# All up units of the feed-forward layers but each layer's first as seven block products

## The chip, the cores and the metric

The kernel runs on one NeuronCore of a Trainium2 chip. The metric is the time of one launch on the device in microseconds: the median of several runs, the profiled execution aside.

## The reference

A trunk of two encoder layers on 512 tokens of width 1024, all in float32. The token mixers (a gated linear recurrence with latent attention in the first layer, differential attention in the second) are not touched here. Each layer ends with a gated feed-forward part of 2816 hidden features:

```python
def swiglu(h, w_gate, w_up, w_down):
    return (jax.nn.silu(h @ w_gate) * (h @ w_up)) @ w_down

for layer in range(DEPTH):                      # DEPTH = 2
    ...
    x = x + mix
    x = x + swiglu(rmsnorm(x, norm_ffn[layer]), ffn_w_gate[layer], ffn_w_up[layer], ffn_w_down[layer])
return rmsnorm(x, final_norm)
```

## The kernel before

**Numbers.** Every float32 operand of a big product is held as two parts, hi and lo, and a product is three matmuls (`mm3`, L335 to L337): hi by hi, the weight's hi by the activation's lo, the weight's lo by the activation's hi. Features lie on partitions and tokens run along a row, so an activation tile is 128 features by 512 tokens.

**Weights.** `weight_plan` is a list of entries in the order of use; an entry is up to 512 rows by 256 columns of a weight matrix, loaded into a tile `raw` (two buffers) by SyncE's DMA queue and split by `_split` (L292 on ScalarE, L293 on VectorE) into `whi` and `wlo` (four buffers each). Asking for entry i with `weight` first writes the splits up to entry i + 2, and each split writes the load of the next free entry behind it. A buffer is written again only when those who read its last content are done: raw is free when both halves of the split have read it, whi and wlo when TensorE has.

**The feed-forward part.** `ffn_hidden` goes over the 22 hidden blocks of 128 features in groups of 8, 8 and 6 (GROUPS). In a group it takes pairs of blocks b, b + 1: first a unit for gate (256 columns), then one for up. Behind each group `projection` multiplies the group's hidden features by their rows of the down weights and adds to the residual (L667). There are two forms of a unit:

- An ordinary unit (`features`) has two PSUM banks. Per entry (two in a unit) it takes two column blocks by four row blocks by three matmuls of 512 tokens: 48 matmuls. Evacuation of up: L1044 (by the norm), L1045 (by the silu of gate), then oph (L343 on ScalarE) and opl (L344 on VectorE), per block of 512.
- A seven-product unit (`seven`) sees weights and activations as two by two blocks and takes seven block products instead of eight (PRODUCTS), each of 128 by 128 by 256 tokens. Per entry that is 7 products by 2 pairs of row blocks by 3 matmuls of 256 tokens, 84 matmuls in a unit. Its weights are split by `_split7`: sums of weight blocks on VectorE (`wsum`, L306 to L308), then hi on ScalarE and lo on VectorE (L314, L315) of both the plain blocks (`whi`, `wlo`, 128x768) and the sums (`shi`, `slo`, 128x1024). The first three products of an entry use the plain blocks, the other four the sums. The products land in four of the eight PSUM banks; the evacuation puts them together (L403 on ScalarE into `tu`, L404 to L408 on VectorE into a tile `cz`), multiplies by the norm (L1034) and, for up, by the silu of gate (L1050), and makes hi and lo of the two blocks (L343 and L346 on ScalarE, L344 and L347 on VectorE). For gate, ScalarE's L1039 is the silu.

Which form a unit takes is decided by `seven(w, b)`:

```python
def seven(w, b):

    return b > 0 if w == "gate" else b % 4 == 2
```

so gate has seven products everywhere but at b = 0, and up at b = 2, 6, 10, 14 and 18. For b = 0 both are ordinary, because the norm is not there yet.

**Order.** TensorE's instructions stand in the order in which the code writes them. Those of the other engines are put in order by the scheduler of the language, from its own idea of when each can run; each engine then works through its list in that order.

Of the kernel before, what the change touches and what calls it, by code (L numbers as in the profile page):

```python
# [49 lines left out]
def weight_plan():  # L50
    plan = []
    for p in range(2):
        for base in (512, 1024, 0, 2048, 1536):
            plan += [("ab_in", k, 4, base + 256 * p, 256) for k in (0, 4)]
    for c in (2560, 2816, 3072):
        plan += [("ab_in", k, 4, c, 256) for k in (0, 4)]
    plan += [("uq", k, 1, 0, 768) for k in range(3)]
    plan += [("ukv", k, 1, 0, 1024) for k in range(2)]
    for k in (0, 4):
        plan += [("ab_out", k, 4, 256 * j, 256) for j in range(4)]  # L60
    plan += ffn_plan(0)
    for hp in range(4):
        for base in (0, 1024, 2048):
            plan += [("c_in", k, 4, base + 256 * hp, 256) for k in (0, 4)]
    for k in (0, 4):
        plan += [("c_out", k, 4, 256 * j, 256) for j in range(4)]
    plan += ffn_plan(1)
    return plan


def seven(w, b):

    return b > 0 if w == "gate" else b % 4 == 2


def ffn_plan(l):
    plan = []
    for g0, gn in GROUPS:
        for b in range(g0, g0 + gn, 2):
            for w in ("gate", "up"):  # L80
                plan += [("seven" * seven(w, b) + w + str(l), k, 4, 128 * b, 256) for k in (0, 4)]
        if l == 0 or g0 + gn < FFN // 128:
            for j in range(4):
                plan += [(f"down{l}", g0 + k, min(4, gn - k), 256 * j, 256) for k in range(0, gn, 4)]
        else:
            for ch in range(2):
                plan += [("down1", g0 + k, 2, 512 * ch, 512) for k in range(0, gn, 2)]
    return plan
# [56 lines left out]
class Kernel:  # L145
# [871 lines left out]
    def ffn_hidden(self, l, g0, gn, xg, stats, sums):  # L1017


        nc = self.nc  # L1020
        hop = self.operand("f", (0, 1))
        parts, make = sums
        for b in range(0, gn, 2):
            zs = []

            def gate(i, ps):
                if not zs:
                    zs.append(self.s4("cz"))
                z = zs[0][:, 1 - i, :]
                nc.vector.tensor_mul(z, ps[:], self.R[:])  # L1030
                nc.scalar.activation(z, z, AF.Silu)

            def by_norm(c):
                nc.vector.tensor_mul(c[:], c[:], self.R[:].unsqueeze(1).broadcast_to([128, 2, 512]))  # L1034

            def gate7(c):
                by_norm(c)
                for i in range(2):
                    nc.scalar.activation(c[:, i, :], c[:, i, :], AF.Silu, scale=2.0 * i - 1.0)  # L1039
                zs.append(c)  # L1040

            def up(i, ps):
                u = self.s2("u")
                nc.vector.tensor_mul(u[:], ps[:], self.R[:])  # L1044
                nc.vector.tensor_mul(u[:], u[:], zs[0][:, 1 - i, :])  # L1045
                self.hi_lo(u[:], *hop(b + i))

            def up7(c):
                by_norm(c)
                nc.vector.tensor_mul(c[:], c[:], zs[0][:])  # L1050
                self.hi_lo(c[:, 1, :], *hop(b))
                self.hi_lo(c[:, 0, :], *hop(b + 1), scale=-1.0)

            if self.R is None:

                held = []

                def norm():
                    self.r = self.rms(stats[0], D)

                def release():
                    self.R = self.spread(self.r)
                    for h in held:
                        gate(*h)

                for m in range(2):
                    make(m)
                yield from self.features(f"gate{l}", 128 * (g0 + b), FULL, xg, lambda *h: held.append(h))
                for m in range(2, 4):
                    make(m)  # L1070
                yield from self.later(self.later(self.features(f"up{l}", 128 * (g0 + b), FULL, xg, up),
                                                 norm, steps=1), release, steps=4)
                continue
            for w, evac, evac7 in (("gate", gate, gate7), ("up", up, up7)):
                if seven(w, g0 + b):
                    yield from self.seven(f"seven{w}{l}", 128 * (g0 + b), parts, evac7)
                else:
                    yield from self.features(f"{w}{l}", 128 * (g0 + b), FULL, xg, evac)
        return hop
# [319 lines left out]
```

## Time and profile before

| | us |
|---|---|
| median of 3 runs | 1308.56 (1308.08 to 1309.05) |
| the profiled execution | 1309.75 |
| its span on the core | 1308.0 |
| TensorE busy | 1285.5 (98%) |
| VectorE busy | 967.9 (74%) |
| ScalarE busy | 612.2 (47%) |
| GpSimd busy | 164.8 (13%) |
| granted clock of TensorE, mean | 0.996 of full |

PE is TensorE's matmuls, PEld its weight loads, DVE VectorE, ACT ScalarE, POOL GpSimd, SP SyncE. The duration of a matmul in a timeline is longer than its distance from the next, since matmuls overlap in the array; VectorE's rows overlap a little too. How long a run of them takes is read from start to start, or from a stretch divided by its instructions.

### The profile page before, as it was taken

How to read it: one execution, taken by the hardware profiler on the slowest of the kernel's cores; microseconds unless marked ns; L12 is line 12 of the kernel's file. 1: busy time of each engine (PE TensorE's matmuls, PEld its weight loads, DVE VectorE, ACT ScalarE, POOL GpSimd, SP SyncE). 2: the span in 40 equal slices, each digit the busy share in tenths (PEclk: the TensorE clock that was granted, in tenths of full speed). 3: DMA queues.
4: the chain of work that ended last, by engine and by line, in shares of the span. 5: the costliest groups of instructions: out<-in, count | busy, mean ns of one | idle time of the engine just before them, and what ended most of it. 6: DMA issues, size and time to landing. Idle time of an engine off the chain costs nothing.

```text
span 1308.0 us, 19724 instructions
## 1 busy us (share of the span) xinstructions
PE 1285.5 (98%) x7746; PEld 1146.3 (88%) x7746; DVE 967.9 (74%) x1575; ACT 612.2 (47%) x1060; POOL 164.8 (13%) x147
## 2 busy tenths in 40 slices
PE   7999999999999999999999999999989999999997
PEld 7898988888799899989988889888879989998996
DVE  4678498646998479748767888887789748865964
ACT  6554464744644234324354566665654323432442
POOL 0222232001200000000035223130310000000002
PEclk9999999999999999999999999999989999999999
DMA  6422123212233333332332221221123333333331
GB/s 197 129 66 65 51 68 107 72 33 56 74 113 114 97 97 98 113 97 83 104 105 81 81 65 49 65 65 50 49 86 108 113 97 97 97 114 97 101 110 65
DMA packets 111745, 115.34 MB, mean 88 GB/s; under 512 B 7786, under 2 KB 107812, under 8 KB 111652
## 3 DMA queue, kind: packets, MB, share of 16 engines
q1 hardware_dynamic: 110324, 112.11, 28.1%
q10 hardware_dynamic: 1328, 1.97, 0.5%
q8 instruction: 61, 1.00, 0.3%
q14 instruction: 32, 0.26, 0.1%
HBM read 111.97 MB, written 2.10 MB: 87 GB/s over the span
## 4 chain that ended last, share of the span: by engine, by line
PE 90%; DVE 3%; issue 3%; ACT 2%; POOL 1%; DMA 0%; POOLq 0%; ACTq 0%
PE mm L335 26%; PE mm L336 26%; PE mm L337 26%; PE o L869 3%; PE lv L734 2%; PE pt L859 1%; PE o L777 1%; PE sc L1205 1%; PE sc L1206 1%; DVE opl L347 1%; DVE wlo L293 1%; PE lv L768 1%; PE bc L469 1%; PE ot L509 0%; DVE xT L667 0%
## 5 line engine op out<-in xcount | busy, mean ns | idle before, releaser
L335 PE MATMUL mm<-oph,whi 128*128 128x512 f32 (+1 forms) x1208 | 452.8, 375 | 1.1 <-ACT whi L292 1.1
L336 PE MATMUL mm<-opl,whi 128*128 128x512 f32 (+1 forms) x1208 | 445.0, 368 | 0.9 <-DVE opl L347 0.9
L337 PE MATMUL mm<-oph,wlo 128*128 128x512 f32 (+1 forms) x1208 | 445.0, 368 | 0.0
L337 PEld LDWEIGHTS mm<-oph,wlo 128*128 128x128 f32 x1208 | 228.9, 189 | 38.4 <-DVE wlo L293 0.2
L336 PEld LDWEIGHTS mm<-opl,whi 128*128 128x128 f32 x1208 | 229.5, 190 | 36.3 <-DVE opl L347 1.3
L335 PEld LDWEIGHTS mm<-oph,whi 128*128 128x128 f32 x1208 | 229.5, 190 | 36.3 <-ACT whi L292 1.5
L292 ACT CAST whi<-raw 128x1024 fp32r<-128x1024 f32 (+1 forms) x130 | 131.2, 1012 | 197.5 <-PE mm L336 130.6
L293 DVE TENSOR_TENSOR wlo<-raw,whi 128x1024 fp32r<-128x1024 f32 (+1 forms) x130 | 155.0, 1195 | 83.5 <-ACT whi L292 83.1
L337 PE MATMUL mm<-th,slo 128*128 128x256 f32 x360 | 101.9, 283 | 0.0
L335 PE MATMUL mm<-th,shi 128*128 128x256 f32 x360 | 101.9, 283 | 0.0
L336 PE MATMUL mm<-tl,shi 128*128 128x256 f32 x360 | 101.9, 283 | 0.0
L314 ACT CAST shi<-wsum 128x1024 fp32r<-128x1024 f32 x60 | 62.4, 1049 | 70.5 <-DVE wsum L308 64.3
L488 POOL TENSOR_TENSOR sq<-sq,sq 128x512 f32<-128x512 f32 x24 | 37.1, 1546 | 441.8 <-ACT sq L494 440.5
L315 DVE TENSOR_TENSOR slo<-wsum,shi 128x1024 fp32r<-128x1024 f32 x60 | 73.3, 1224 | 15.2 <-ACT shi L314 15.1
L667 DVE TENSOR_TENSOR xT<-xT,mm 128x512 f32<-128x512 f32 x72 | 49.1, 684 | 37.6 <-PE mm L337 37.5
L851 ACT ACTIVATE p<-sc,mx 128x512 f32<-128x512 f32 x80 | 55.0, 691 | 45.6 <-DVE mx L849 41.0
L335 PE MATMUL mm<-whi,oph 128*128 128x256 f32 (+1 forms) x246 | 75.4, 306 | 0.0
L337 PE MATMUL mm<-whi,opl 128*128 128x256 f32 (+1 forms) x246 | 74.1, 301 | 0.0
L336 PE MATMUL mm<-wlo,oph 128*128 128x256 f32 (+1 forms) x246 | 74.0, 301 | 0.0
L314 ACT CAST whi<-raw 128x768 fp32r<-128x768 f32 x60 | 50.0, 834 | 41.6 <-PE mm L336 25.2
L335 PEld LDWEIGHTS mm<-th,shi 128*128 128x128 f32 x360 | 69.1, 192 | 0.0
L336 PEld LDWEIGHTS mm<-tl,shi 128*128 128x128 f32 x360 | 69.1, 192 | 0.0
(241 smaller groups left out, 2329.6 us busy)
## 6 DMA issues: line engine op xcount, KB each, us to landing
raw<-in_ffn_w_down_dram SPq DMA_DIRECT2D x42, 512.0 KB, 3.4
raw<-in_ffn_w_gate_dram SPq DMA_DIRECT2D x80, 256.0 KB, 3.0
raw<-in_ab_w_in_dram SPq DMA_DIRECT2D x24, 512.0 KB, 3.8
raw<-in_ffn_w_up_dram SPq DMA_DIRECT2D x24, 512.0 KB, 3.7
raw<-in_c_w_in_dram SPq DMA_DIRECT2D x24, 512.0 KB, 3.6
raw<-in_ffn_w_up_dram SPq DMA_DIRECT2D x40, 256.0 KB, 2.9
xs<-in_x_dram SPq DMA_DIRECT2D x8, 512.0 KB, 5.1
raw<-in_ab_w_out_dram SPq DMA_DIRECT2D x8, 512.0 KB, 3.4
```

Of the source, the lines that this page charges most:

```text
L292: self.nc.scalar.copy(h, r)
L293: self.nc.vector.tensor_sub(l, r, h.bitcast(F32))
L314: nc.scalar.copy(hi, src)
L315: nc.vector.tensor_sub(lo, src, hi.bitcast(F32))
L335: mm(ps, lhsT=lhs[0], rhs=rhs[0], start=first, stop=False)
L336: mm(ps, lhsT=lhs[0], rhs=rhs[1], start=False, stop=False)
L337: mm(ps, lhsT=lhs[1], rhs=rhs[0], start=False, stop=last)
L488: self.nc.gpsimd.tensor_add(acc[0][:], acc[0][:], s[:])
L667: nc.vector.tensor_add(self.x(j), self.x(j), ps)
L734: nc.tensor.matmul(ps[:, sl], lhsT=kc[:, sl], rhs=qc[:, sl], start=True, stop=True)
L851: nc.scalar.activation(p[:], ps, AF.Exp, bias=m[:], scale=scale, accum_out=l)
L869: self.nc.tensor.matmul(po[:, tb * 128:(tb + 1) * 128], lhsT=pt[:, s * 128:(s + 1) * 128], rhs=V[:, s // 2, c:c + 128], start=s == 0, stop ...
```

## The change

`seven` takes only b, and is true for b > 0, for up as for gate: in each layer the up units at b = 4, 8, 12, 16 and 20 become seven-product units as well. Their weight entries are loaded as two transfers of 256 KB in place of one of 512 KB and split by `_split7`.

```diff
-def seven(w, b):
-
-    return b > 0 if w == "gate" else b % 4 == 2
+def seven(b):
+
+    return b > 0
...
-                plan += [("seven" * seven(w, b) + w + str(l), k, 4, 128 * b, 256) for k in (0, 4)]
+                plan += [("seven" * seven(b) + w + str(l), k, 4, 128 * b, 256) for k in (0, 4)]
...
-                if seven(w, g0 + b):
+                if seven(g0 + b):
                     yield from self.seven(f"seven{w}{l}", 128 * (g0 + b), parts, evac7)
```

TensorE has ten times 84 matmuls in place of ten times 48. With more seven-product units the scheduler also orders VectorE's and ScalarE's lists otherwise around those that were there. In the rows that follow, an instruction is named by its line, its operation, the tile it writes and those it reads, with the numbers of the buffers.

First place: VectorE in the second group of the first layer, around the start of the evacuation of the last gate unit (b = 14). slo885 and slo891 are the sums' lo parts for the two entries of the up unit behind it. Before:

```order
L307 TENSOR_TENSOR wsum881_4940<-wsum881_4940,raw866_4858 128x2x128
L1045 TENSOR_TENSOR u876_4931<-u876_4931,cz856_4832 128x512
L308 TENSOR_TENSOR wsum881_4940<-wsum881_4940,raw866_4858 128x2x128
L306 TENSOR_TENSOR wsum887_4996<-raw872_4897 128x2x256
L344 TENSOR_TENSOR opl875_4916<-u876_4931,oph874_4915 128x512
L307 TENSOR_TENSOR wsum887_4996<-wsum887_4996,raw872_4897 128x2x128
L315 TENSOR_TENSOR slo885_4947<-wsum881_4940,shi884_4946 128x1024
L308 TENSOR_TENSOR wsum887_4996<-wsum887_4996,raw872_4897 128x2x128
L315 TENSOR_TENSOR wlo889_5001<-raw872_4897,whi888_5000 128x768
L315 TENSOR_TENSOR slo891_5003<-wsum887_4996,shi890_5002 128x1024
L404 TENSOR_TENSOR cz893_5052<-tu894_5053,mm877_4936 128x256
```

After, the same tiles are slo912 and slo918:

```order
L347 SCALAR_TENSOR_TENSOR opl903_5114<-cz899_5102,oph902_5113 128x512
L306 TENSOR_TENSOR wsum908_5123<-raw892_5000 128x2x256
L306 TENSOR_TENSOR wsum914_5179<-raw898_5057 128x2x256
L307 TENSOR_TENSOR wsum908_5123<-wsum908_5123,raw892_5000 128x2x128
L307 TENSOR_TENSOR wsum914_5179<-wsum914_5179,raw898_5057 128x2x128
L308 TENSOR_TENSOR wsum908_5123<-wsum908_5123,raw892_5000 128x2x128
L308 TENSOR_TENSOR wsum914_5179<-wsum914_5179,raw898_5057 128x2x128
L404 TENSOR_TENSOR cz920_5235<-tu921_5236,mm904_5119 128x256
L405 TENSOR_TENSOR tu921_5236<-tu921_5236,mm906_5121 128x256
L315 TENSOR_TENSOR slo912_5130<-wsum908_5123,shi911_5129 128x1024
L315 TENSOR_TENSOR slo918_5186<-wsum914_5179,shi917_5185 128x1024
```

Both slo stood ahead of the gate unit's evacuation and stand now behind its L404 and L405, which read the banks of that gate unit.

Second place: ScalarE at the end of that group, where the last up unit (b = 14) is evacuated and the down projection begins. oph909 (after: oph936) is the hi part of that unit's hidden blocks. Before:

```order
L403 COPY tu907_5165<-mm896_5064 128x256
L292 CAST whi916_5213<-raw905_5120 128x1024
L343 CAST oph909_5175<-cz906_5164 128x512
L346 ACTIVATE oph909_5175<-cz906_5164 128x512
L292 CAST whi921_5247<-raw915_5187 128x1024
L292 CAST whi924_5277<-raw918_5217 128x1024
```

After:

```order
L403 COPY tu934_5348<-mm923_5247 128x256
L1039 ACTIVATE cz920_5235<-cz920_5235 128x512 x2
L292 CAST whi940_5366<-raw929_5255 128x1024
L292 CAST whi943_5396<-raw932_5303 128x1024
L292 CAST whi948_5430<-raw942_5370 128x1024
L343 CAST oph936_5358<-cz933_5347 128x512
L346 ACTIVATE oph936_5358<-cz933_5347 128x512
```

The fifth split of the down projection (whi921, now whi948) stood behind the two halves of oph and stands now ahead of them.

Third place: VectorE at the same point. Before:

```order
L405 TENSOR_TENSOR tu907_5165<-tu907_5165,mm898_5066 128x256
L406 TENSOR_TENSOR uu908_5166<-tu907_5165,mm897_5065 128x512
L407 TENSOR_TENSOR cz906_5164<-uu908_5166,mm897_5065 128x256
L408 TENSOR_TENSOR cz906_5164<-uu908_5166,mm899_5067 128x2x256
L1034 TENSOR_TENSOR cz906_5164<-cz906_5164,R620_3215 128x1024
L1050 TENSOR_TENSOR cz906_5164<-cz906_5164,cz893_5052 128x1024
L344 TENSOR_TENSOR opl910_5176<-cz906_5164,oph909_5175 128x512
L347 SCALAR_TENSOR_TENSOR opl910_5176<-cz906_5164,oph909_5175 128x512
L293 TENSOR_TENSOR wlo922_5248<-raw915_5187,whi921_5247 128x1024
```

After:

```order
L405 TENSOR_TENSOR tu934_5348<-tu934_5348,mm925_5249 128x256
L406 TENSOR_TENSOR uu935_5349<-tu934_5348,mm924_5248 128x512
L407 TENSOR_TENSOR cz933_5347<-uu935_5349,mm924_5248 128x256
L408 TENSOR_TENSOR cz933_5347<-uu935_5349,mm926_5250 128x2x256
L293 TENSOR_TENSOR wlo941_5367<-raw929_5255,whi940_5366 128x1024
L1034 TENSOR_TENSOR cz933_5347<-cz933_5347,R620_3215 128x1024
L293 TENSOR_TENSOR wlo944_5397<-raw932_5303,whi943_5396 128x1024
L1050 TENSOR_TENSOR cz933_5347<-cz933_5347,cz920_5235 128x1024
L293 TENSOR_TENSOR wlo949_5431<-raw942_5370,whi948_5430 128x1024
L344 TENSOR_TENSOR opl937_5359<-cz933_5347,oph936_5358 128x512
L347 SCALAR_TENSOR_TENSOR opl937_5359<-cz933_5347,oph936_5358 128x512
```

The chain from the banks to opl ran without a break and holds now three splits of down weights. The first group of the first layer, and the first two of the second, stand in the same way at all three places; the third group has no split of down weights between its last L405 and its last opl.

## Rows read from the trace of the kernel before

**Rows 1.** The page, part 1 (busy time by engine) and part 4 (chain).

```profile
PE 1285.5 (98%) x7746; PEld 1146.3 (88%) x7746; DVE 967.9 (74%) x1575; ACT 612.2 (47%) x1060; POOL 164.8 (13%) x147
...
PE 90%; DVE 3%; issue 3%; ACT 2%; POOL 1%; DMA 0%; POOLq 0%; ACTq 0%
```

**Rows 2.** Busy times by stretch, first layer's feed-forward part; its first row names the columns.

```profile
core 0: us, PE busy (x) PEld busy (x) DVE busy (x) ACT busy (x) POOL busy (x), PEclk, DMA share, GB/s
357.23:387.47 30.24, 30.24 (x254) 30.23 (x253) 29.21 (x46) 14.59 (x21) 0.00 (x0) 1.00 0.41 122
462.07:472.15 10.08, 10.08 (x86) 10.07 (x85) 5.87 (x11) 3.43 (x5) 0.00 (x0) 1.00 0.17 54
472.15:483.05 10.90, 10.90 (x50) 9.01 (x49) 10.85 (x16) 5.20 (x7) 0.00 (x0) 1.00 0.42 128
...
534.27:544.35 10.08, 10.08 (x87) 10.08 (x86) 7.21 (x10) 4.58 (x6) 0.00 (x0) 1.00 0.49 158
544.35:587.89 43.54, 43.54 (x194) 36.04 (x193) 23.06 (x29) 10.19 (x11) 0.00 (x0) 1.00 0.33 97
```

**Rows 3.** Timeline of DVE, second group: start, duration, instruction, idle before and its end.

```profile
485.95 0.95 DVE L315 TENSOR_TENSOR wlo<-raw,whi 128x768 fp32r<-128x768 f32 x1
486.82 0.69 DVE L344 TENSOR_TENSOR opl<-u,oph 128x512 fp32r<-128x512 f32 x1
...
494.24 0.42 DVE L407 TENSOR_TENSOR cz<-uu,mm 128x256 f32<-128x256 f32 x1
494.57 0.69 DVE L408 TENSOR_TENSOR cz<-uu,mm 128x512 f32<-128x512 f32 x1
495.17 1.22 DVE L315 TENSOR_TENSOR slo<-wsum,shi 128x1024 fp32r<-128x1024 f32 x1
496.30 1.23 DVE L1034 TENSOR_TENSOR cz<-cz,R 128x1024 f32<-128x1024 f32 x1
```

**Rows 4.** Timeline of DVE around the end of the second group, at 544.35.

```profile
528.40 1.23 DVE L315 TENSOR_TENSOR slo<-wsum,shi 128x1024 fp32r<-128x1024 f32 x1
...
543.83 0.42 DVE L405 TENSOR_TENSOR tu<-tu,mm 128x256 f32<-128x256 f32 x1
544.28 0.69 DVE L406 TENSOR_TENSOR uu<-tu,mm 128x512 f32<-128x512 f32 x1
545.00 0.42 DVE L407 TENSOR_TENSOR cz<-uu,mm 128x256 f32<-128x256 f32 x1
545.34 0.68 DVE L408 TENSOR_TENSOR cz<-uu,mm 128x512 f32<-128x512 f32 x1
...
549.22 0.69 DVE L344 TENSOR_TENSOR opl<-cz,oph 128x512 fp32r<-128x512 f32 x1 [0.69 <-ACT oph L343]
```

**Rows 5.** Timeline of ACT at the same place.

```profile
549.83 1.05 ACT L292 CAST whi<-raw 128x1024 fp32r<-128x1024 f32 x1
```

**Rows 6.** The page: costliest groups (part 5) and DMA issues (part 6).

```profile
L314 ACT CAST shi<-wsum 128x1024 fp32r<-128x1024 f32 x60 | 62.4, 1049 | 70.5 <-DVE wsum L308 64.3
...
L314 ACT CAST whi<-raw 128x768 fp32r<-128x768 f32 x60 | 50.0, 834 | 41.6 <-PE mm L336 25.2
...
raw<-in_ffn_w_down_dram SPq DMA_DIRECT2D x42, 512.0 KB, 3.4
...
raw<-in_ffn_w_up_dram SPq DMA_DIRECT2D x40, 256.0 KB, 2.9
```

**Rows 7.** Timeline of PE at two of its waits, one in each layer.

```profile
340.33 0.50 PE L336 MATMUL mm<-opl,whi 128*128 128x512 f32 x1 [0.90 <-DVE opl L347]
...
962.68 0.80 PE L469 MATMUL bc<-cst,rt 128*128 128x128 f32 x2 [4.67 <-POOL rt L461]
```

**Rows 8.** Busy times by stretch at these two waits; columns as in rows 2.

```profile
338.00:342.00 4.00, 3.10 (x14) 2.24 (x13) 4.00 (x5) 2.52 (x4) 1.73 (x1) 1.00 0.43 131
...
963.00:965.00 2.00, 2.00 (x10) 1.90 (x10) 0.00 (x0) 0.15 (x1) 0.00 (x0) 0.50 0.00 0
...
967.00:969.00 2.00, 2.00 (x9) 1.54 (x9) 1.31 (x4) 1.62 (x3) 0.00 (x0) 0.86 0.00 0
```

## The prediction

> **What bounds the kernel now.** I read part 1 and the chain of the page first [rows 1]: TensorE is busy 98% of a span of 1308.0 us, 90% of the chain that ended last is PE, VectorE (DVE) is busy 74%, ScalarE (ACT) 47%. Then the feed-forward part unit by unit in the busy times by stretch [rows 2]. A unit there is 256 hidden columns of gate or of up. An ordinary unit is 48 matmuls of 512 columns in 10.90 us, 0.227 us each; a seven-product unit is 84 of 256 columns in 10.08 us, 0.120 us each (the view's own counts are one or two higher, since it counts those that reach over an edge). In both PE is busy for the whole stretch: it waits for nobody. But DVE is busy 29.21 of 30.24 us where three seven-product units stand in a row (gate, up, gate at 357), 10.85 of 10.90 in the unit at 472, and only 7.21 of 10.08 and 23.06 of 43.54 in the last unit of a group and in the down projection behind it. So PE is the bound, and in the middle of a group DVE is nearly one too.
>
> **What the change takes off PE.** Five up units in each layer (b = 4, 8, 12, 16, 20) turn from ordinary into seven-product units: ten times 10.90 - 10.08 = 0.82 us, **-8.2 us**, if PE goes on waiting for nobody. The first units of the layers stay ordinary, and no DMA is added in bytes (two transfers of 256 KB for one of 512 KB).
>
> **What it puts on DVE.** I price DVE's instructions by the distance from one start to the next where they stand close [rows 3]: 0.60 us for 128x512 (L306, L406, L408, L344, L347), 0.34 for 128x256 (L307, L308, L404, L405, L407), 0.87 for the 128x768 wlo, 1.13 for 128x1024 (slo, L293, L1034, L1050). Splitting one weight entry then costs 0.60 + 2 x 0.34 + 0.87 + 1.13 = 3.28 us in place of 1.13, and a unit has two entries. Evacuating an up unit costs 3 x 0.34 + 2 x 0.60 + 2 x 1.13 + 2 x 0.60 = 5.7 in place of 6 x 0.60 = 3.6; a gate unit 3.4. A pair of two seven-product units therefore asks 4 x 3.28 + 5.7 + 3.4 = 22.2 us of DVE in 2 x 10.08 = 20.16 us of PE. Before, every other pair had an ordinary up unit, 2 x 3.28 + 2 x 1.13 + 3.6 + 3.4 = 15.8 us in 20.98, and DVE caught up there. That breathing space is gone, up to the last unit of a group, whose DVE work is cheap since the next splits are those of down weights.
>
> ACT gets 0.83 + 1.05 us per entry [rows 6] for 1.05, at 47% busy: nothing by itself. Its place in the queue matters, below.
>
> **Where PE then waits.** The queues are in order, so I walked the changed order at the two places where the rows moved.
>
> First place: the last gate unit of groups 1 and 2 (b = 6 and 14). Before, slo of the following up unit's first entry was written ahead of that gate unit's evacuation; it ended at 529.6 [rows 4], and PE needs it 18 + 2 matmuls of 0.120 us into the up unit that begins at 534.27, at 536.7: 7 us to spare. Now slo912 stands behind L404 and L405 of the gate unit's evacuation, which wait for the gate unit's own end. Counted from L405 of the up unit before (released 0.52 us before that unit's end, as 543.83 against 544.35 [rows 2, 4]) to the end of slo912, DVE has L405, L406, wlo, slo, L407, L408, wlo, L1034, L1050, L344, L347, twice L306, L307 and L308, L404, L405 and slo912: 0.34 + 0.60 + 0.87 + 1.13 + 0.34 + 0.60 + 0.87 + 1.13 + 1.13 + 0.60 + 0.60 + 1.20 + 0.68 + 0.68 + 0.34 + 0.34 + 1.13 = 12.6 us, so it ends 12.1 us after that unit's end. PE needs it at 10.08 + 2.40 = 12.5. Without any idle it is met by 0.4. But in this stretch DVE waits 0.7 us for ACT's oph before L344, as it did before [rows 4]; some 0.4 for wlo916, whose raw lands 0.4 + 2.9 us after its buffer came free and is cast in 0.83 more [rows 6], 4.2 us in which DVE has 3.9 of other work; and 0.1 for ACT's shi (1.05 us of cast [rows 6] against 1.02 of other work). That makes the wait 0.8 us if DVE comes to the stretch on time. It doesn't quite: from L405 of the gate unit three units earlier the order holds six splits less one slo (18.6), three evacuations as of a gate (10.1) and one product with its hi and lo (2.3), 31.0 us of DVE in 30.24, 0.7 over, and the three units at 357 show that DVE idles up to 1.0 in such a run [rows 2]; I take 0.4 of it, a lag of 1.1. **1.9 us of PE waiting**, from 0.8 (on time) to 3.0 (the whole 1.0 idle, and some more for a transfer).
>
> Second place: the handover to the down projection behind those groups. PE starts down with hidden blocks 0 to 3 and needs oph and opl of block 6 in its second entry, 31 matmuls of 0.227 us in: 7.03 us after the unit's end. Before, the last evacuation had DVE to itself and opl was there 5.6 us after the unit's end (549.22 + 0.69 against 544.35 [rows 4]), 1.5 to spare. Now three splits of down weights (wlo941, wlo944, wlo949) stand inside that evacuation on DVE, and on ACT the cast whi948 stands before oph936. whi has four buffers; whi948 takes that of whi927, which PE reads in down's first entry to its 23rd matmul, 5.2 us after the unit's end. And raw942 takes the buffer of raw929, read by wlo941: L405 to L408 and wlo941 end 0.45 + 0.72 + 0.34 + 0.60 + 1.23 - 0.52 = 2.8 us after the unit's end (the first steps one behind the other, as at 543.83 to 545.34 [rows 4]), the transfer lands 3.4 later [rows 6], at 6.2. So whi948, a cast of 1.05 us [rows 5], runs from 6.25 to 7.3, wlo949 from 7.35 to 8.5, L344 to 9.15: **2.1 us of waiting**, where before there was none. If the transfer is early, PE's own reading sets whi948, and it is 5.25 + 1.05 + 1.15 + 0.65 + 0.1 - 7.03 = 1.2; with a lag of 0.5 on DVE, 2.6.
>
> Both rows of places stand the same in groups 1 and 2 of both layers, so four times: 4 x (1.9 + 2.1) = **+16.0**. Group 3: no lag is left over (its last evacuation has no split of down weights behind L405), the chain takes 5.6 us, and 0.60 more for the second block, as at 544, against needs at 24 + 1 and 24 + 4 matmuls, 5.67 and 6.35 us: 0 (up to 1 with lag) in layer 0; in layer 1 transposes and 10.9 us of other matmuls come first, 0.
>
> **Sum:** -8.2 + 16.0 = +7.8. The profiled execution took 1309.75 us, 1.75 of it outside the span; the median of the runs is 1308.56, 1.19 below it. On the median: **1316.4 us**. With the ends of the two waits, 4 x (0.8 + 1.2) = 8.0 and 4 x (3.0 + 2.6) = 22.4, it is 1308.4 to 1322.8.
>
> **The rivals.** (1) *The cover holds.* DVE keeps its 7 us of lead and the handover stays inside its 1.5 us: all 8.2 us come in, 1300.4. For it: PE waits for nothing now even where DVE is at 97%. Against it: the order moved slo912 and opl937 behind things that can't be early. It decides at lags under zero at both places. 8 in 100. (2) *Only the handover waits*, the first place being met: 4 x (1.2 to 2.1) - 8.2, from -3.4 to +0.2: 1305.2 to 1308.8. It needs DVE idle under 0.4 us in 12.6, less than the three units at 357 show. 16 in 100. (3) *PE's clock falls in the new waits.* After an idle of 4.67 us, to 962.68, the granted clock was 0.50, the lower of its two levels, for the next 4 us and 0.86 on the mean of the 2 us behind, so that PE's work there lost about 2.3 us (half of 4.0 and 0.14 of 2.0); after an idle of 0.90 at 340 it stayed at 1.00 [rows 7, 8]. My waits of 1.9 and 2.1 lie nearer the second, and the first of them comes in two pieces, for shi and for slo. If it falls at one place in each of the four groups, 4 x 2.3 more: 1325.6; 11 in 100, with all ways in which the waits are longer than I bound them. (4) *A steeper gain on PE.* By the 0.120 and 0.227 us the gain is 0.82 a unit, and I hold it so. The Trainium skill (TensorE: Matmul & The Clock Gate, Part 1, "Wait — 56ns, not 53.3ns?") states a step of the columns at 2.4 GHz plus about 2.5 ns: 84 x 109.2 ns against 48 x 215.8 ns, an estimate of 1.19 us a unit, 11.9 in all, and with my waits 1312.7. The stretches of both forms measure otherwise, some 13 ns over the columns' time at either width, which weighs more on the narrow form; 1 in 100. That the change does less than it says is out: the order has ten times 36 matmuls more.
>
> **How the numbers follow.** The forecast has 64 in 100, 1316.4, of which 9 lie under 1311.2 and 5 over 1323. A measurement of this kernel tells 0.2% from no change, 2.6 us: faster is under 1305.9, slower over 1311.2. Faster: rival 1 and a third of rival 2, 13. Same: the rest of rival 2 and the forecast's low end, 19 to 20. Slower: 68. For 8 in 10 the range goes from the low end of rival 2, 1305, to 1323.
>
> **What would show it.** Units of 10.08 us at b = 4, 8, 12, 16, 20: the gain. In the waits, PE idle of 1 to 3 us until slo L315 (with shi on ACT just ahead of it) in the last up unit of groups 1 and 2, and until opl L344 some 7 us into the down projections, eight places in all, and none in group 3. ACT's cast ahead of oph waiting for PE or for down's transfer. I am wrong if slo comes in time (L405 of the last gate unit not delayed), if whi948 finds its transfer long landed, or if the clock row shows 0.50 behind a wait.

## The result, and the profile after

The changed kernel takes **1325.31 us** (median of 4 runs, 1323.92 to 1328.34) against 1308.46 before: a ratio of **1.0132 (1.0118 to 1.0146)**, 1.3% slower. The forecast was 1316.4 with a range of 1305 to 1323: the sign was right, the loss of 16.9 us is more than twice the 7.8 that the sum gave, and the time lies outside the range. The profiled execution is the slowest of the four, 1328.34 us with a span of 1326.6, 18.6 more than before.

Parts 1 and 4 of the page of the changed kernel, to be read beside [rows 1]:

```profile
PE 1286.0 (97%) x8106; PEld 1160.4 (87%) x8106; DVE 1027.6 (77%) x1685; ACT 632.3 (48%) x1090; POOL 164.3 (12%) x147
...
PE 65%; DVE 21%; DMA 4%; ACT 4%; issue 4%; POOL 1%; SPq 0%; ACTq 0%; POOLq 0%; DVEq 0%
```

PE's busy time hardly moved although 360 matmuls were added (ten times 84 in place of 48). The chain tells the story: PE held 90% of it and holds 65%; DVE went from 3% to 21%, DMA and ACT to 4% each. The added units themselves are as fast as forecast. Busy times by stretch (columns as in rows 2): six seven-product units of group 3 in a row, then three stretches behind the wait at 543.66 and one behind the wait at 1036.67.

```profile
598.80:659.27 60.47, 60.47 (x505) 60.47 (x504) 55.34 (x86) 27.24 (x38) 0.00 (x0) 1.00 0.31 95
...
544.00:546.00 2.00, 2.00 (x15) 2.00 (x14) 1.97 (x4) 1.04 (x1) 0.00 (x0) 0.69 0.81 286
546.00:548.00 2.00, 2.00 (x11) 2.00 (x11) 2.00 (x3) 1.05 (x1) 0.00 (x0) 0.50 0.00 0
548.00:550.00 2.00, 2.00 (x18) 2.00 (x17) 1.81 (x3) 0.42 (x2) 0.00 (x0) 0.95 0.57 177
...
1038.00:1040.00 2.00, 2.00 (x12) 2.00 (x12) 1.97 (x4) 1.59 (x2) 0.00 (x0) 0.57 0.27 96
```

504 matmuls in 60.47 us is 10.08 us a unit and no wait (PEclk, the third number from the end, is the granted clock). PE's timeline in group 2 of layer 0 has the two places of the forecast (the number in brackets is the idle time ahead of the row, and what ended it):

```profile
542.40 0.39 PE L335 MATMUL mm<-th,shi 128*128 128x256 f32 x1 [2.13 <-ACT shi L314]
...
543.66 0.39 PE L337 MATMUL mm<-th,slo 128*128 128x256 f32 x1 [0.76 <-DVE slo L315]
...
560.82 0.51 PE L335 MATMUL mm<-oph,whi 128*128 128x512 f32 x1 [0.91 <-ACT oph L343]
562.17 0.50 PE L336 MATMUL mm<-opl,whi 128*128 128x512 f32 x1 [0.84 <-DVE opl L344]
```

The first pair is the last up unit, waiting for shi and then slo; the second is the down projection, waiting for the last evacuation. ACT's timeline shows why oph is late there: a cast of a down entry stands ahead of it and waits 4.96 us for its transfer.

```profile
559.20 1.05 ACT L292 CAST whi<-raw 128x1024 fp32r<-128x1024 f32 x1 [4.96 <-DMA raw<-in_ffn_w_down_dram]
560.16 0.61 ACT L343 CAST oph<-cz 128x512 fp32r<-128x512 f32 x1
```

Counted by the distance from one matmul's start to the next, less the usual one, PE loses 3.4, 3.4, 2.6 and 3.0 us at the first place of the four groups (12.4), and 2.4, 2.3, 2.2 and 2.5 at the handovers (9.4). Behind two of the first waits the granted clock fell to the lower of its two levels, in the stretches at 546 and 1038 above (0.50, and 0.57 on the mean of 2 us): matmuls of 256 columns then start 0.213 us apart in place of 0.120, and 1.5 and 1.3 us are lost (2.8). Layer 1 has 0.8 us more in the transposes behind its last unit and 0.6 in its first gate unit, where matmuls run at the lower clock for 6.1 us behind the wait that ends at 972.06, and for 4.9 before. (It also has a new wait of 0.9 us in its attention's output projection, but PE's next wait there is shorter by as much, so that it costs nothing; see the last section.) Together -8.2 + 12.4 + 9.4 + 2.8 + 1.4 = 17.8, against 18.6 measured between the two spans. Of the 0.8 that are left, 0.3 lie in the first 16 us, where the two kernels are the same; the other 0.5 I have not placed.

### The profile page after: what moved, and what is told of

It is laid out like the page before. It is cut to its first block, busy times and chain, and to the rows that moved or that the text cites. A ratio compares the mean times of both kernels' runs of the same rounds, so it can differ in the third digit from the quotient of the medians.

```text
span 1326.6 us, 20638 instructions
## 1 busy us (share of the span) xinstructions
PE 1286.0 (97%) x8106; PEld 1160.4 (87%) x8106; DVE 1027.6 (77%) x1685; ACT 632.3 (48%) x1090; POOL 164.3 (12%) x147
## 4 chain that ended last, share of the span: by engine, by line
PE 65%; DVE 21%; DMA 4%; ACT 4%; issue 4%; POOL 1%; SPq 0%; ACTq 0%; POOLq 0%; DVEq 0%
PE mm L337 17%; PE mm L336 17%; PE mm L335 17%; DVE slo L315 3%; PE o L869 3%; DMA raw<-in_ffn_w_up_dram 2%; PE lv L734 2%; DVE wsum L306 2%; DVE wlo L315 2%; DVE cz L1034 1%; DVE wlo L293 1%; DMA raw<-in_ffn_w_down_dram 1%; PE pt L859 1%; DVE opl L347 1%; DVE wsum L307 1%
## 5 line engine op out<-in xcount | busy, mean ns | idle before, releaser
L335 PE MATMUL mm<-oph,whi 128*128 128x512 f32 (+1 forms) x1128 | 414.1, 367 | 4.9 <-ACT oph L343 3.8
L336 PE MATMUL mm<-opl,whi 128*128 128x512 f32 (+1 forms) x1128 | 406.5, 360 | 4.9 <-DVE opl L344 3.4
L337 PE MATMUL mm<-oph,wlo 128*128 128x512 f32 (+1 forms) x1128 | 405.9, 360 | 0.0
L335 PE MATMUL mm<-th,shi 128*128 128x256 f32 x480 | 137.1, 286 | 7.2 <-ACT shi L314 7.2
L337 PE MATMUL mm<-th,slo 128*128 128x256 f32 x480 | 137.4, 286 | 3.0 <-DVE slo L315 3.0
L336 PE MATMUL mm<-tl,shi 128*128 128x256 f32 x480 | 136.7, 285 | 0.0
L315 DVE TENSOR_TENSOR slo<-wsum,shi 128x1024 fp32r<-128x1024 f32 x80 | 97.3, 1220 | 23.1 <-ACT shi L314 22.5
L335 PEld LDWEIGHTS mm<-th,shi 128*128 128x128 f32 x480 | 93.1, 194 | 8.1 <-ACT shi L314 8.1
L337 PEld LDWEIGHTS mm<-th,slo 128*128 128x128 f32 x480 | 93.1, 194 | 3.8 <-DVE slo L315 3.8
L315 DVE TENSOR_TENSOR wlo<-raw,whi 128x768 fp32r<-128x768 f32 x80 | 75.8, 952 | 11.5 <-ACT whi L314 11.5
```

Source lines behind the costliest of these rows:

```text
L315: nc.vector.tensor_sub(lo, src, hi.bitcast(F32))
L335: mm(ps, lhsT=lhs[0], rhs=rhs[0], start=first, stop=False)
L336: mm(ps, lhsT=lhs[0], rhs=rhs[1], start=False, stop=False)
L337: mm(ps, lhsT=lhs[1], rhs=rhs[0], start=False, stop=last)
```

## The experiments

**Group 3 alone** (the diff is against the kernel before). Are the added units free where nothing waits?

```diff
-    return b > 0 if w == "gate" else b % 4 == 2
+    return b > 0 if w == "gate" else b % 4 == 2 or b >= 16
```

> Only the up units of b = 16 and 20 (group 3) are turned into seven-product units beside those of the kernel before, four units in all. My theory (the waits come only where a last unit of groups 1 and 2 follows three seven-product units; each added unit itself takes 10.08 us in place of 10.90): 1308.5 - 4 x 0.82 = 1305.2, up to 1306.2 if the transposes behind the last unit of layer 1 wait 1 us as they do in the changed kernel; no wait for slo L315 in group 3. Rival (every added unit costs its share of the loss, 16.8 / 10 = 1.7 us, through load on VectorE, the transfers or the clock): 1308.5 + 4 x 1.7 = 1315.3.

Measured: 1308.49 us (1306.75 to 1308.95), ratio 0.9997 (0.9988 to 1.0007). Neither theory: 3.3 us of gain don't show. The trace has no wait for slo, but a handover wait in layer 0, which the changed kernel doesn't have at this place. Timeline of PE in the down projection behind group 3, and of DVE ahead of it:

```profile
654.20 0.49 PE L335 MATMUL mm<-oph,whi 128*128 128x512 f32 x1 [0.47 <-ACT oph L343]
654.92 0.50 PE L336 MATMUL mm<-opl,whi 128*128 128x512 f32 x1 [0.23 <-DVE opl L344]
```

```profile
648.18 0.69 DVE L293 TENSOR_TENSOR wlo<-raw,whi 128x512 fp32r<-128x512 f32 x1 [0.26 <-ACT whi L292]
648.79 0.41 DVE L405 TENSOR_TENSOR tu<-tu,mm 128x256 f32<-128x256 f32 x1
```

The group ends at 648.10. L405 could start 0.5 us ahead of that; it starts 0.7 us behind, because the wlo of a down entry stands ahead of it and waits 0.26 us for its cast. PE loses 1.24 us there by the distances of its matmuls. By the rows 2.0 of the 3.3 us are then left, and the median shows none of them: the interval reaches to a gain of 1.6 us, and the runs spread over 2.2. What takes the rest isn't shown. So "each added unit gains 0.82" held on PE in the trace, and "group 3 costs nothing" did not.

**The handover's order.** The third down entry's splits are queued behind the last oph and opl (i1 and i2 are the instructions of up7 that write them):

```diff
...
+                if g0 + b in (6, 14):
+                    self.behind = (i1, i2)
...
+                    for ins in self.behind:
+                        es.enter_context(self.tc.issue_after(ins.ins))
+                    self._split()
...
```

> The changed kernel, but the splits of the third down entry (and of those behind it) of groups 1 and 2 are queued behind oph and opl of the group's last evacuation, on ScalarE and on VectorE. My theory (the handover waits, 2.24 to 2.45 us at four places in the trace of the changed kernel, come from that order): opl is there about 5.6 us after the unit's end, as before, against a need at 7.03, so 4 x 2.35 = 9.4 us go: 1325.3 - 9.4 = 1316, and the waits of the first place stay at 2.7 to 3.4 each. Rival (VectorE's lag is the cause, whatever the order; the down splits that now come later make PE wait at the third entry instead): 1321 to 1325.

Measured: 1315.98 us (1314.82 to 1317.78), ratio 1.0057 (1.0042 to 1.0072): 9.3 us back, as the theory said. The timeline of DVE at the same place (the evacuation's lines are 7 higher in this kernel) has L405's successor L412 0.5 us ahead of the unit's end (548.76), where it had waited for PE, and opl 5.5 us later, where the changed kernel had 9.0 (552.40 to 561.42):

```profile
548.25 0.42 DVE L412 TENSOR_TENSOR tu<-tu,mm 128x256 f32<-128x256 f32 x1 [2.00 <-PE mm L344]
...
553.72 0.69 DVE L351 TENSOR_TENSOR opl<-cz,oph 128x512 fp32r<-128x512 f32 x1 [0.69 <-ACT oph L350]
```

In the feed-forward groups PE's waits are now those for shi and slo alone, 2.0 to 3.6 us at each of the four first places.

**The sums on GpSimd**, without and with that order. This takes 5.1 us of work per pair off DVE; L306 is moved as L307 and L308 are here.

```diff
...
-        nc.vector.tensor_add(t[:, :, 2, :], t[:, :, 0, :], r[:, :, 2, :])
-        nc.vector.tensor_add(t[:, :, 3, :], t[:, :, 2, :], r[:, :, 0, :])
+        nc.gpsimd.tensor_add(t[:, :, 2, :], t[:, :, 0, :], r[:, :, 2, :])
+        nc.gpsimd.tensor_add(t[:, :, 3, :], t[:, :, 2, :], r[:, :, 0, :])
```

> The changed kernel with the three sums of every seven-product weight entry (L306 to L308) on GpSimd in place of VectorE. VectorE then has 22.2 - 4 x 1.28 = 17.1 us of work for a pair of units of 20.16. My theory (the first place's wait comes from VectorE's load): no wait for shi or slo in the last up unit of groups 1 and 2, and with oph now ahead of the third down cast at most 0.5 us at each of the four handovers: 1308.5 - 8.2 = 1300.3 to 1302.3. Rival 1 (GpSimd is too slow: 1.55 + 2 x 0.8 = 3.2 us an entry, by its rows of 128x512 and 128x256 elsewhere, in a period of 5.04, and the sums come late to shi): a wait for shi in many units, over 1325. Rival 2 (GpSimd and VectorE hold each other up in SBUF; the Trainium skill, Profiling: Reading And Analyzing Traces, says that moving work between these two might not help since they share a port): VectorE's rows grow, by 0.3 us per entry and more, and the waits stay: 1315 to 1325.

(The page of the Trainium skill that this text means is titled Perfetto Trace Analysis; the rule is in its section "Optimizing Scalar/DVE Operations". The 0.8 us for 128x256 on GpSimd is no row's: in the trace of the kernel before, its adds of that size take 1.05.)

> Both edits: the sums on GpSimd, and the third down entry's splits behind the last evacuation. My theory: no wait at either place, all ten gains of 0.82 us come in: 1300.3 to 1301.3. Rivals as for the sums on GpSimd alone: over 1315.

Measured: 1350.33 us, ratio 1.0308 (1.0287 to 1.0329), and 1338.36 us, ratio 1.0226 (1.0194 to 1.0259). Both are worse than the changed kernel. The costliest groups of the page of the first (mean ns of one behind the comma), then one row of its DVE timeline; the last row is the slo group of the changed kernel's page:

```profile
L306 POOL TENSOR_TENSOR wsum<-raw 128x512 f32<-128x512 f32 x80 | 125.0, 1564 | 310.8 <-DMA raw<-in_ffn_w_gate_dram 223.5
...
L315 DVE TENSOR_TENSOR slo<-wsum,shi 128x1024 fp32r<-128x1024 f32 x80 | 119.4, 1497 | 52.1 <-ACT shi L314 52.1
...
L314 ACT CAST shi<-wsum 128x1024 fp32r<-128x1024 f32 x80 | 83.2, 1045 | 124.1 <-POOL wsum L308 114.5
...
L307 POOL TENSOR_TENSOR wsum<-wsum,raw 128x256 f32<-128x256 f32 x80 | 103.3, 1305 | 1.7
```

```profile
532.44 2.32 DVE L1034 TENSOR_TENSOR cz<-cz,R 128x1024 f32<-128x1024 f32 x1
```

```profile
L315 DVE TENSOR_TENSOR slo<-wsum,shi 128x1024 fp32r<-128x1024 f32 x80 | 97.3, 1220 | 23.1 <-ACT shi L314 22.5
```

What both rivals named shows; the time is in the first one's range (over 1325). An entry's sums take 1.56 + 1.31 + 0.97 = 3.8 us on GpSimd (L306, L307, L308) in a period of 5.04, and shi waits for them. (PE itself waits for shi four times, 9.8 us in all, and for slo nine times, 6.4 us: not in many units.) And DVE's instructions grow beside them: L1034 of 1.22 us took 2.32 at 532.44 and 2.0 on the mean of the 7 that have a sum on GpSimd beside them for over half of their time; slo took 1.50 on the mean for 1.22. Instructions that read a PSUM bank kept their times: 26 of the 40 L405 have a sum beside them and take 0.41, as do 20 of the 40 L406, which take 0.69. The Trainium skill (SBUF — State Buffer, "Who interferes with whom") states it so: a DVE instruction with two SBUF inputs contends with a GpSimd instruction that reads SBUF, and one with a single SBUF input doesn't; the rows agree. As a test of "DVE's load sets the first wait" this pair says nothing, since it hardly lowered that load: DVE is busy for 1005.1 us in the first of the two, for 1027.6 in the changed kernel. Which of the two rivals costs how much isn't told apart.

**Later need.** In the last up unit of groups 1 and 2 PE takes the products without sums of both entries first, then those with shi, then those with slo. The rows of DVE and ACT keep their order.

```diff
...
+            order = [(e, p, m, x) for e in (0, 1) for p in PRODUCTS if p[0][0] == 0 for m in range(2) for x in range(3)]
+            order += [(e, p, m, x) for xs in ((0, 1), (2,)) for e in (0, 1) for p in PRODUCTS if p[0][0] == 1
+                      for m in range(2) for x in xs]
...
```

> The changed kernel with the same order on VectorE and ScalarE, but in the last up unit of groups 1 and 2 TensorE takes the products of both weight entries that need no sums first, then those with shi of both, then those with slo: shi is needed 4.32 us into the unit in place of 2.16, slo 8.2 in place of 2.4. My theory (the first place's wait is VectorE's lateness against that need: in group 2 of layer 0 shi came 4.4 us into the unit): the first wait falls from 2.7 to 3.4 us to 0 to 0.5 at each of the four places, and the clock no longer falls there. The unit then ends 3 us earlier while VectorE still has the two slo and two wlo ahead of its evacuation, about 1 us late, and the handover wait grows from 2.35 to about 3.4: net 2.1 x 4 = 8.4 us and 1 to 2 of clock: 1325.3 - 9 to 10 = 1315.5 (1314 to 1318). Rival (all of it is given back at the handover, since VectorE's work behind it is a fixed chain): 1323 to 1325.

Measured: 1329.72 us, ratio 1.0153 (1.0136 to 1.0170): a miss, on the side of the rival and beyond it. The first wait went as expected, to 0 at three places and 0.46 at the fourth. But at the handover PE now waits as follows (timeline of PE, then two stretches with the columns of rows 2):

```profile
560.77 0.80 PE L335 MATMUL mm<-oph,whi 128*128 128x512 f32 x1 [4.63 <-ACT oph L343]
562.11 0.80 PE L336 MATMUL mm<-opl,whi 128*128 128x512 f32 x1 [0.54 <-DVE opl L344]
```

```profile
562.00:564.00 2.00, 1.89 (x5) 1.50 (x6) 0.66 (x2) 0.00 (x0) 0.00 (x0) 0.50 0.60 192
564.00:566.00 2.00, 2.00 (x6) 1.62 (x5) 0.69 (x1) 0.00 (x0) 0.00 (x0) 0.50 0.20 70
```

opl is awaited until 562.11 here and until 562.17 in the changed kernel. From the start of group 2 to the start of opl's L344 it is 93.3 us here (468.07 to 561.38) and 94.0 there (467.40 to 561.42), although the last unit ends 3.8 us earlier here (549.15 for 552.93). Timeline of DVE, in the changed kernel and then here:

```profile
552.40 0.42 DVE L405 TENSOR_TENSOR tu<-tu,mm 128x256 f32<-128x256 f32 x1 [2.00 <-PE mm L337]
```

```profile
550.95 0.41 DVE L418 TENSOR_TENSOR tu<-tu,mm 128x256 f32<-128x256 f32 x1
...
554.40 1.23 DVE L293 TENSOR_TENSOR wlo<-raw,whi 128x1024 fp32r<-128x1024 f32 x1 [1.27 <-ACT whi L292]
```

In the changed kernel L405 waited for PE. Here the same instruction (L418) comes 1.8 us behind the unit's end without a wait, since DVE is late itself, and a split of down weights behind it then waits for its cast, whose transfer took 4.8 us from issue to landing (3.5 there). In the four groups opl is there only 0.7 to 2.0 us earlier, counted from the group's start, and most of what PE doesn't wait at the first place it waits at the second: 19 us in all, for 22 in the changed kernel. The wait at the handover is now longer, and the clock falls behind it at all four handovers, where 6 to 12 matmuls of 512 columns take 0.427 us or more in place of 0.227: some 8 us, against 2.8 by the clock in the changed kernel.

**Later need and the handover's order together**, and then also down's second entry by pairs of hidden blocks:

```diff
+            pairs = w.startswith("down") and k0 in (4, 12)
+            for i, k in ([(i, k) for kk in (k0, k0 + 2) for i in range(2) for k in (kk, kk + 1)] if pairs else
...
```

> The later sums and the third down entry's splits behind the last evacuation, both. My theory (the two waits add up and no third one lies behind them): L405 about 1 us late, opl some 6.4 us behind the unit's end against a need at 7.03, so no wait at either place: 1300.3 to 1302.5. Rival (VectorE's backlog must come out somewhere: 2 us for each pair of units stay as a wait): 4 x 2 more, 1308 or above.

> As the kernel before in this list, and in the second entry of each down block of groups 1 and 2 TensorE takes hidden blocks 4 and 5 for both output halves ahead of blocks 6 and 7, so that oph and opl of the last unit are needed 12 x 0.227 / 2 = 1.4 us later. My theory: nothing waits at either place with 1.4 us to spare, 1300.3 to 1301.5; if it differs from the kernel without this edit, by what is left of the handover wait there, 0 to 2 us in all. Rival (some 2 us for each pair stay, whatever the order): 1308.

Measured: 1306.69 us, ratio 0.9983 (0.9974 to 0.9993), and **1303.14 us, ratio 0.9958 (0.9943 to 0.9973)**. The rival's 1308 is out in both, but both also miss the theory's range, and the two differ by 3.5 us where I allowed 0 to 2. In the first, PE still loses 0.3 to 1.1 us at each handover and 1.5 in group 3 of layer 0, which I hadn't counted. Timeline of PE in the first and of DVE in the second, group 2 of layer 0:

```profile
550.27 0.50 PE L343 MATMUL mm<-opl,whi 128*128 128x512 f32 x1 [0.23 <-DVE opl L351]
```

```profile
543.36 0.41 DVE L427 TENSOR_TENSOR tu<-tu,mm 128x256 f32<-128x256 f32 x1
...
548.83 0.69 DVE L351 TENSOR_TENSOR opl<-cz,oph 128x512 fp32r<-128x512 f32 x1 [0.69 <-ACT oph L350]
```

L405's successor, L427 here, starts at 543.36 for a unit that ends at 541.78, some 2.1 us later than it could (its bank is ready 0.52 us ahead of the end), with two slo and two wlo ahead of it; so the backlog is still there, and reading blocks 6 and 7 1.4 us later hides what of it was left. The handover waits of groups 1 and 2 are gone in the second; the 1.5 us in group 3 of layer 0 are still there.

**Less work on DVE.** The norm's multiply is left out of the evacuation of every seven-product up unit, so that this kernel computes less than the others:

```diff
             def up7(c):
-                by_norm(c)
```

> The changed kernel without the norm's multiply (L1034) in the evacuation of the seven-product up units, a part of the computation that is left out: 1.13 us of VectorE less in each pair, 21.1 for 20.16 us of TensorE. The order at the first place is the same. My theory (the first wait is VectorE's lag plus its work behind L405): that work is 1.13 shorter and the lag some 0.8 to 1.1 less, so the wait falls from 3.1 to about 1 us (0.5 to 2); at the handover opl now stands ahead of the fifth down entry's split and comes 1.13 earlier, 0 to 1 in place of 2.35: 1325.3 - 8 - 6 = 1311 (1308 to 1316). Rival (ScalarE's casts or the transfers set shi and whi, not VectorE): 1323 to 1325.

Measured: 1302.42 us, ratio 0.9950 (0.9936 to 0.9965), 8.6 us under what I expected. The rival is out: the casts and transfers are the same, and of the eight places one has a wait of 0.4 and one of 0.8 us. The timeline of DVE shows L405 of the last gate unit at that unit's end, where the changed kernel has it 4.4 us late (541.80 for a unit that ends at 537.96):

```profile
531.22 0.42 DVE L405 TENSOR_TENSOR tu<-tu,mm 128x256 f32<-128x256 f32 x1
531.58 2.36 DVE L315 TENSOR_TENSOR slo<-wsum,shi 128x1024 fp32r<-128x1024 f32 x2
```

It is no clean dose: with the shorter evacuation one slo and one wlo also moved ahead of L405 of the up unit before. How much of the wait's end came from the 1.13 and how much from the order isn't told apart.

**Group 3's handover** queued in the same way, on top of the kernel of 1303.14, and **the last up unit ordinary** in the changed kernel (its diff, the second, is against the kernel before):

```diff
-                if g0 + b in (6, 14):
+                if g0 + b in (6, 14) or (g0 + b == 20 and l == 0):
```

```diff
-    return b > 0 if w == "gate" else b % 4 == 2
+    return b > 0 if w == "gate" else b > 0 and b not in (6, 14)
```

> The kernel with the later sums, the down splits behind the last evacuation and the block pairs in the down entries (1303.1), and the same queueing of the third down entry's splits behind the last evacuation of group 3 in layer 0. There the trace showed 1.51 us of waiting for oph and opl, since the fourth down entry's wlo stood ahead of L405, which came 1.5 us late. My theory: L405 comes 0.5 us ahead of the unit's end and opl 5.6 behind it, against a need at 5.67, as in the changed kernel's own trace: 1303.1 - 1.4 = 1301.7 (1301 to 1302.5). Rival (the evacuation's own chain is too long there in any order): 1303.

> The changed kernel with the last up unit of groups 1 and 2 (b = 6 and 14) ordinary: of the ten added units six are left on balance against the kernel before, 6 x 0.82 = 4.9 us. My theory (both waits need a seven-product unit at the end of the group: an ordinary one asks 2 x 1.13 of VectorE for its splits in place of 2 x 3.28, and nothing of it stands behind L404 and L405): no wait at the first place, 0 to 1 us at each handover, and the 1.2 to 1.5 us in group 3 of layer 0 that the partial kernel showed: 1308.5 - 4.9 + 1.5 = 1305 (1303.5 to 1308). Rival (the lag of the three pairs before it comes out at the handover all the same, 2 us at each of four): 1311 to 1313.

Measured: **1302.72 us (1302.24 to 1304.12), ratio 0.9955 (0.9942 to 0.9967)**, and 1305.93 us, ratio 0.9977 (0.9967 to 0.9986). The second is what the theory said: no wait at the first place or at the handovers of groups 1 and 2, and 1.5 us in group 3 of layer 0. In the first, the timeline of DVE in group 3 has L405 (L427) waiting for PE again, and PE waits for nothing there; by the medians that is worth 0.4 us of the 1.4, which misses the forecast and is less than the runs of either kernel spread. Busy times of the seven-product units of groups 1 and 2 of layer 0 in it (columns as in rows 2; starts 0.120 us apart would make 60.48 and 80.64):

```profile
645.89 0.42 DVE L427 TENSOR_TENSOR tu<-tu,mm 128x256 f32<-128x256 f32 x1 [2.00 <-PE mm L344]
```

```profile
356.87:417.82 60.95, 60.74 (x506) 60.53 (x504) 57.44 (x90) 27.20 (x38) 0.00 (x0) 1.00 0.31 96
461.37:542.38 81.01, 80.87 (x673) 80.67 (x672) 74.27 (x115) 35.38 (x48) 0.00 (x0) 1.00 0.30 92
```

This kernel beats both, by 6.1 us and 22.6: three quarters of the 8.2 us come in once next to nothing waits.

## Why the prediction was right in kind and wrong in size

**Right.** The gain (units of 10.08 us); the two places, in all four groups; who is awaited there (shi and slo, then oph and opl); the cause at the handover (the experiment on its order gave back 9.3 of the 9.4 us). The handover's wait was 2.2 to 2.5 for a forecast of 2.1, inside its bounds.

**The term that was mis-sized** is the first place: 1.9 us with a bound of 3.0, and 2.6 to 3.4 measured (3.1 on the mean). This is the step that failed. Its sum had three parts: the lag of L405 of the up unit before, the work from there to slo's end, and DVE's idle time on the way. The timeline of DVE in the changed kernel, in group 2 and then in group 1 of layer 0, and ACT's cast in group 1:

```profile
529.11 0.41 DVE L405 TENSOR_TENSOR tu<-tu,mm 128x256 f32<-128x256 f32 x1
529.55 0.69 DVE L406 TENSOR_TENSOR uu<-tu,mm 128x512 f32<-128x512 f32 x1
...
533.67 0.96 DVE L315 TENSOR_TENSOR wlo<-raw,whi 128x768 fp32r<-128x768 f32 x1 [0.50 <-ACT whi L314]
...
537.71 0.69 DVE L344 TENSOR_TENSOR opl<-cz,oph 128x512 fp32r<-128x512 f32 x1 [0.69 <-ACT oph L343]
...
541.80 0.41 DVE L405 TENSOR_TENSOR tu<-tu,mm 128x256 f32<-128x256 f32 x1
542.38 2.36 DVE L315 TENSOR_TENSOR slo<-wsum,shi 128x1024 fp32r<-128x1024 f32 x2 [0.17 <-ACT shi L314]
```

```profile
397.68 0.41 DVE L405 TENSOR_TENSOR tu<-tu,mm 128x256 f32<-128x256 f32 x1
...
403.65 0.96 DVE L315 TENSOR_TENSOR wlo<-raw,whi 128x768 fp32r<-128x768 f32 x1 [1.90 <-ACT whi L314]
...
412.36 2.36 DVE L315 TENSOR_TENSOR slo<-wsum,shi 128x1024 fp32r<-128x1024 f32 x2 [0.17 <-ACT shi L314]
```

```profile
402.78 0.83 ACT L314 CAST whi<-raw 128x768 fp32r<-128x768 f32 x1 [3.25 <-DMA raw<-in_ffn_w_up_dram]
```

| part, us | forecast | layer 0, group 2 | layer 0, group 1 | layer 1, group 1 | layer 1, group 2 |
|---|---|---|---|---|---|
| lag of L405 | 1.1 | 1.8 | 0.4 | 0.0 | 1.3 |
| idle on the way | 1.2 | 1.4 | 2.8 | 2.2 | 1.4 |
| work to slo's end | 12.6 | 13.1 | 13.1 | 13.2 | 13.1 |
| wait: the sum less 0.52 and 12.48 | 1.9 | 3.3 | 3.3 | 2.4 | 2.8 |

The work is each case's stretch to the end of the first of the two slo (529.11 to 543.61 and 397.68 to 413.58 in the two timelines) less its idle; PE's own count is 0.1 to 0.2 higher, since the matmul behind each of the two waits starts late too. The work is 0.5 longer than forecast, since I priced rows by the distance to the next one where the next doesn't need the result; where it does (L405 to L406, L1034 to L1050), it is 0.44 for 0.34 and 1.25 for 1.13. The idle for wlo's cast was put at 0.4 and is 0.5 to 1.9. I took 3.3 us from the buffer's release to the transfer's landing; by the trace it is, to the cast, 3.6 in group 2 (release at 529.18, cast at 532.81), 4.5 in group 1 of layer 1, and 5.0 in group 1 of layer 0 (397.74 to 402.78). A part of that is plain: such an entry is loaded by two transfers that SyncE issues one behind the other, the second 0.42 us later. Why one took 1.4 us longer than another isn't settled. Where DVE was more on time, it stood longer at that cast, so that lag and this idle together come to 2.3 us in both groups of layer 0; in layer 1 they come to 1.4 and 1.8, and the wait is shorter by about as much. PE waits for shi first, then slo, and the later of them decides, as forecast. The place of slo behind L404 and L405 is not what held it: L405 at 541.80 comes 4.4 us after its bank was ready, without a wait, and DVE then idles 0.17 us until shi is cast. What held both is the queue ahead, with the sums of both entries in it. No run puts the sums and slo further ahead in the queue with DVE's work left as it is, so what the order alone costs there isn't shown.

**The addition of the two places** stood on a condition that I hadn't seen. 2.1 us at the handover was right only because PE came there late: without the first wait it would have been the 4.0 to 5.9 us that the later need showed. The two waits are one chain, seen twice: in the changed kernel's order of the queues mending the second alone gave 9.3 us back, and mending the first alone gave nothing.

**The clock**, a rival at 11 in 100 with a fall in each group, came at two of the four first waits, for 1.5 and 1.3 us where I had priced 2.3. The sum had nothing for it, and 0.50 behind a wait was one of the prediction's own signs of being wrong. The wait at 412.4 (2.42 and 1.04 us from start to start) left it at 1.00, and the shorter one at 1035.4 (1.54 and 1.04) didn't: what I argued from, the length of a wait against 4.67 and 0.90 [rows 7, 8], does not tell it.

**Left out**: 0.8 us in the transposes of layer 1, which I held for 0, and 0.6 us of the first gate unit in that layer. These 1.4 us, 4.8 of the first places, 1.0 of the handovers and 2.8 of the clock make 10.0, against the 10.8 by which the profiled 1328.34 is over 1309.75 + 7.8. The median is 3.0 under that execution, and the four runs show mean clocks of 0.994 to 0.996: how often the clock falls is one thing that differs between them.

## What to carry to other kernels

Before a vector engine at nine tenths gets more work, walk its queue to the last consumer, with the distance between dependent rows, not between independent ones, and with the whole time from a buffer's release to the cast behind its transfer. Two waits of one engine behind the same queue are not two costs: find out which of them is left if the other is gone, since mending only the first can move most of it into one longer wait, behind which the clock fell here. Often the cheaper cure is the consumer's order (read last what comes last) and the place of prefetch work behind, not ahead of, what is awaited next.

## What the runs showed of the hardware that I had not expected

The 0.9 us in layer 1's output projection is a meeting of DVE and GpSimd, and which of the two is held up differs from trace to trace. The row of L347 there and GpSimd's add of squares beside it, and PE's next wait for GpSimd, in the changed kernel; then the first two (L354 and L495) in the kernel with the handover's order:

```profile
956.50 1.86 DVE L347 SCALAR_TENSOR_TENSOR opl<-xT,vec,oph 128x512 fp32r<-128x512 f32 x1
956.52 1.29 POOL L488 TENSOR_TENSOR sq<-sq,sq 128x512 f32<-128x512 f32 x1 [1.69 <-ACT sq L494]
...
972.06 0.80 PE L469 MATMUL bc<-cst,rt 128*128 128x128 f32 x2 [3.75 <-POOL rt L461]
```

```profile
950.03 0.74 DVE L354 SCALAR_TENSOR_TENSOR opl<-xT,vec,oph 128x512 fp32r<-128x512 f32 x1
950.05 1.87 POOL L495 TENSOR_TENSOR sq<-sq,sq 128x512 f32<-128x512 f32 x1 [1.70 <-ACT sq L501]
```

The two start 0.02 us apart in both. In the changed kernel DVE's instruction takes 1.86 us and GpSimd's 1.29, in the other kernel 0.74 and 1.87. All twelve traces show one of these two pictures, eight the first and four, the kernel before among them, the second, although no edit touched this stretch. In the first PE waits for opl and then less for GpSimd, 3.75 us at 972.06 for 4.67 in the kernel before [rows 7], so that nothing is lost on balance: a wait that is new in a trace can be paid back by the next one.

And a wait can cost half as much again behind its end: after the 4.63 us of waiting that ended at 560.77, with later sums, the granted clock was 0.50 in the stretches from 562 to 566, and the matmuls behind the wait lost some 2.5 us.
